# A decoder layer with Strassen weight sums: the copies that begin the sums get a queue of their own, a lead of 24 and other rates

## The chip, the cores and the metric

The kernel runs on one core of one Trainium2 chip. The metric is the device time of one execution in microseconds (us); lower is better. Each time is the median of several executions of the same program. The durations below come from one execution that the hardware profiler recorded.

## The reference

One layer of a decoder, in float32, for one sequence of 512 tokens of width 1024. A combined input projection gives queries, keys and values for three attention mixers and three gate vectors; the branches are projected, gated, summed and projected once more; after a layer norm come a squared-ReLU MLP (1024 to 4096 to 1024) and a gated input embedding, and a second layer norm. Cut to what matters here:

```python
def mixer(x, w_in, ...):
    proj = x @ w_in                                  # 1024 x 8192 columns, 3072 of them gates
    (da_q, da_k, da_v, sb_q, sb_k, sb_v, dl_q, dl_k, dl_v, gates) = jnp.split(proj, ...)
    o_da = diff_attention(...)                       # 4 heads, two softmax maps, T5 bias
    o_sb = stick_breaking_attention(...)             # 8 heads
    o_dl = dilated_attention(...)                    # 3 groups x 4 heads, T5 bias
    g = jax.nn.sigmoid(gates).reshape(B, S, 3, D)
    merged = g[:, :, 0] * (o_da @ w_branch_da) + g[:, :, 1] * (o_sb @ w_branch_sb) \
           + g[:, :, 2] * (o_dl @ w_branch_dil)
    return merged @ w_out

x = layer_norm(ALPHA * x + mixer(x, ...), ln1_g, ln1_b)
c = jnp.square(jax.nn.relu(x @ w_up)) @ w_down
ple = jax.nn.sigmoid(x @ w_ple_gate) * (p @ w_ple)
x = layer_norm(ALPHA * x + c + ple, ln2_g, ln2_b)
```

## The kernel before

**Products.** Every large product is made in split precision: a weight block of 128 x 1024 floats is loaded into `raw`, ScalarE (ACT) rounds it to `wh` (L232), VectorE (DVE) forms the rest `wl = raw - wh` (L235), and TensorE (PE) makes three matmuls with them. There are 4 buffers of `raw` and 7 of `wh` and of `wl`.

**Items.** The work is a list of 312 items; an item is the matmuls of one or of a few blocks and the evacuation of their result. The items run in the order: projections for q, k and v (items 0 to 58, with the attention heads interleaved into them by `step()`), the three gates (59 to 100), the three branch projections (101 to 124), the output projection, embedding gate and embedding (from 125 on, `wout_at`), and then the MLP, in eight groups of up-projection and seven of down-projection. In the loop at the end of `trunk` each item calls `pump`, which starts loads and splits as far ahead as the buffers allow.

**Strassen sums.** Gates, embedding gate and most of the MLP use Strassen-Winograd's scheme: seven products in place of eight. Four of the seven weight operands are sums of blocks. They are not made by an engine but by transfers between DRAM buffers named `total`: `totals()` lists, for each set of four blocks (23 sets), four plain copies of 512 KB (`total<-in_...`, issued on SyncE's queue, SP) and four accumulating transfers (`total<-in_...` or `total<-total`, issued on GpSimd's queue, POOL), 92 copies and 92 additions in all. `add()` (L165) takes the next entry of one list, `sums`, in which copies and additions of a set stand mixed. The loop calls `add()` at a rate: each item adds its `size` to `due[0]`, and each time that reaches `rate` one entry is issued (L1572 to L1577). An addition also waits for a recent cast of a weight (`casts[0]`), so that they don't bunch. `fill()` (L186) issues the loads; before it loads a `total` it issues what is still missing of it.

**Queues.** SP's queue is in order and carries all loads of weights (`raw`), the copies and most other loads. POOL's queue is in order too and carries the additions, the loads and stores of the bias tables, and a few small power operations (L1357, L591). A scheduler places the instructions of each engine; an instruction with `tc.issue_after(i)` stands behind `i` in the order.

**Bias tables.** `tables()` loads three one-hot tables (`oh`, 66 KB each, L1142 to L1144), PE multiplies them with the bias table (L1109), the results go to DRAM (`rv`) and come back shifted (`sh`). It is started at item 13.

Of the kernel before, what the change touches and what calls it, by code (L numbers as in the profile page):

```python
# [13 lines left out]
OP = mybir.AluOpType  # L14
# [38 lines left out]
def trunk(tc, a, out):  # L53
    nc = tc.nc
    es = ExitStack()
    with es:
        big = es.enter_context(tc.tile_pool(name="big", bufs=64))
        ring = es.enter_context(tc.tile_pool(name="ring", bufs=1))
        one = es.enter_context(tc.tile_pool(name="one", bufs=1))
# [7 lines left out]
        def nm(s):  # L67
            uid[0] += 1
            return f"{s}_{uid[0]}"
# [68 lines left out]

        RING, RAW = 7, 4
        ORDERED, AHEAD = 17, 4  # L140
        loads, sums, chunks, placed = [], deque(), [], []
        st = {"dma": 0, "split": 0}

        def load(src, w, own=False):
# [4 lines left out]
        def totals(quads):  # L149

            def new():
                return dram.tile([P, 1024], F32, name=nm("total"), tag=nm("total"), bufs=1)

            t = [[new() for _ in range(4)] for _ in quads]
            for o, i, more in ((0, 0, False), (2, 1, False), (0, 1, True), (2, 3, True), (1, 3, False), (3, 2, False)):
                for (q, x) in zip(quads, t):
                    sums.append((x[o], q[i], more))
            for o in (1, 3):
                for x in t:
                    sums.append((x[o], x[0 if o == 1 else 1][:, :], True))  # L160
            return [{1: q[0], 2: q[2], 3: q[3], 4: x[3], 5: x[0], 6: x[1], 7: x[2]} for q, x in zip(quads, t)]

        casts = deque(maxlen=3)

        def add():  # L165
            if not sums:
                return
            t, s, more = sums.popleft()
            if not more:
                wide = [x.rearrange("(a b) m -> a (b m)", b=4) for x in (t[:, :], s)]  # L170
                nc.sync.dma_start(*wide)
                return
            i = nc.gpsimd.dma_start(t, s, accum_op=OP.add, max_dma_last_dim=2048)  # L173
            tc.add_manual_dep(getattr(i, "ins", i), casts[0].name, mybir.DependencyInfo(
                mybir.DependencyClass.Sync, mybir.DependencyReason.DATA), reason="one sum at a time")

        def chunk_of(s):
            c = {"from": s, "w": s["w"]}
# [7 lines left out]
        def fill():  # L186
            while st["dma"] < len(loads):
                s = loads[st["dma"]]
                while any(t is s["src"] for t, _, _ in sums):
                    add()  # L190
                if not s["own"]:
                    if len(placed) >= RAW and placed[-RAW]["uses"]:
                        break
                    placed.append(s)
                if s["own"]:
                    s["raw"] = slot("rawx")[:, :s["w"]]
                else:
                    r = ring.tile([P, 1024], F32, name=nm("raw"), tag="raw", bufs=RAW)
                    s["raw"] = r[:, :s["w"]]
                if 0 < st["dma"] < ORDERED:  # L200
                    with tc.issue_after(st["load"]):
                        i = nc.sync.dma_start(s["raw"], s["src"])
                else:
                    i = nc.sync.dma_start(s["raw"], s["src"])
                st["load"] = getattr(i, "ins", i)
                if st["dma"] == AHEAD:

                    tc.add_manual_dep(st["load"], st["warm"].name, mybir.DependencyInfo(
                        mybir.DependencyClass.Sync, mybir.DependencyReason.DATA), reason="first loads alone")
                st["dma"] += 1  # L210
# [165 lines left out]
        at = {}  # L376
# [130 lines left out]
        gates_at = len(items)  # L507
# [55 lines left out]
        first_branch = len(items)  # L563
# [490 lines left out]
        wout_at = len(items)  # L1054
# [83 lines left out]
        def tables():  # L1138
            nonlocal tab_g0, tab_g1, tab_g2
            oh = [slot("oh") for _ in range(3)]  # L1140
            ohd = a["onehot"]
            nc.gpsimd.dma_start(oh[0][:33, :], ohd[:, 0:512])  # L1142
            nc.gpsimd.dma_start(oh[1][:33, :], ohd[:, 512:1024])
            nc.gpsimd.dma_start(oh[2][:33, :], ohd[:, 1024:1536])  # L1144
# [398 lines left out]
        for n, it in enumerate(items):  # L1543
# [20 lines left out]
            if n == 13:  # L1564
                pending.append(tables())
# [3 lines left out]
                da_tables()  # L1569
            if n == DA_TABS + 4:  # L1570
                turn_da()
            if n >= 7 and not wout_at + 4 <= n < wout_at + 22:  # L1572
                due[0] += it["size"]
                rate = 2.3 if n < gates_at else 4.5 if n < first_branch else 3
                while due[0] >= rate:
                    due[0] -= rate
                    add()  # L1577
# [116 lines left out]
```

## Time and profile before

| | us |
|---|---|
| median of 3 executions | 1088.29 (1086.98 to 1091.54) |
| the profiled execution, whole | 1088.46 |
| its span, first to last instruction | 1086.8 |
| PE busy in the span | 1052.2 (97%) |
| DVE, ACT, POOL busy | 753.3, 559.1, 105.3 |
| mean granted clock of PE | 0.991 |
| transfers on SP's queue (q1) | 188.15 MB |
| transfers on POOL's queue (q0) | 50.57 MB |

PE is busy nearly throughout, so what remains to be had lies in its few idle stretches and in stretches at a lower clock. The profile lists what each engine waited for; the windows view gives the busy time of each engine, the granted clock and the share of time that the 16 DMA engines were busy, stretch by stretch.

### The profile page before, as it was taken

What the parts mean: (1) busy time and instruction counts of PE and PEld (TensorE: products, weight loads), DVE (VectorE), ACT (ScalarE), POOL (GpSimd) and SP (SyncE); (2) the same over time, 40 slices, a digit from 0 to 9 for tenths busy, and PEclk for the clock granted to TensorE, in tenths of its full rate; (3) what the DMA queues carried; (4) which work ended last, traced back from release to release, by engine and by line L of the source; (5) the groups of instructions that cost most, each with busy time, mean ns of one, the idle gap of its engine ahead of it and who ended that gap; (6) DMA issues with size and microseconds to landing.
All of it is one profiled execution on the core that took longest, in us unless ns stands there. A gap on an engine that the chain in (4) does not pass through costs nothing.

```text
span 1086.8 us, 14845 instructions
## 1 busy us (share of the span) xinstructions
PE 1052.2 (97%) x5503; PEld 899.4 (83%) x5503; DVE 753.3 (69%) x1306; ACT 559.1 (51%) x906; POOL 105.3 (10%) x130
## 2 busy tenths in 40 slices
PE   8999899999999999999999999999999999899997
PEld 5888588999888887788888888878989988778985
DVE  5987367655434656897666675987888667577786
ACT  6665344443332445688654232565856635547551
POOL 0001210110120101011101100100110001000000
PEclk9999899999999999999999999999999999999999
DMA  7676583966888667586989888369999979797622
GB/s 271 205 194 182 162 243 124 266 175 174 219 246 215 173 194 214 197 249 212 262 279 253 231 259 265 117 187 299 285 263 289 298 219 297 258 251 240 218 92 78
DMA packets 73112, 240.58 MB, mean 221 GB/s; under 512 B 8506, under 2 KB 11466, under 8 KB 71568
## 3 DMA queue, kind: packets, MB, share of 16 engines
q1 hardware_dynamic: 46496, 188.15, 47.4%
q0 software_dynamic: 25968, 50.57, 26.3%
q8 instruction: 43, 0.70, 0.3%
q10 hardware_dynamic: 576, 0.92, 0.2%
q14 instruction: 29, 0.24, 0.1%
HBM read 237.48 MB, written 98.59 MB: 309 GB/s over the span
## 4 chain that ended last, share of the span: by engine, by line
PE 79%; DMA 7%; DVE 6%; issue 5%; ACT 3%; POOL 0%; SPq 0%; DVEq 0%; ACTq 0%; POOLq 0%
PE mm L85 5%; PE mm L84 5%; PE mm L86 5%; PE mm L822 4%; PE mm L824 4%; PE mm L823 4%; PE mm L340 3%; PE mm L342 3%; PE mm L341 3%; PE at L430 3%; PE at L428 3%; PE at L431 3%; DMA raw<-total 2%; DVE wl L235 2%; PE mm L548 2%
## 5 line engine op out<-in xcount | busy, mean ns | idle before, releaser
L235 DVE TENSOR_TENSOR wl<-raw,wh 128x1024 fp32r<-128x1024 f32 x245 | 297.2, 1221 | 130.0 <-ACT wh L232 128.0
L232 ACT CAST wh<-raw 128x1024 fp32r<-128x1024 f32 x245 | 256.0, 1050 | 235.8 <-PE mm L85 61.2
L84 PE MATMUL mm<-xhT,wh 128*128 128x512 f32 x304 | 121.0, 398 | 0.0
L86 PE MATMUL mm<-xhT,wl 128*128 128x512 f32 x304 | 120.0, 395 | 0.0
L85 PE MATMUL mm<-xlT,wh 128*128 128x512 f32 x304 | 119.9, 394 | 0.0
L173 POOL DMA_DIRECT2D total<-total x46 | 40.8, 907 | 379.6 <-ACT wh L232 236.7
L822 PE MATMUL mm<-XH,wh 128*128 128x256 f32 x256 | 73.2, 286 | 4.0 <-ACT wh L232 2.1
L824 PE MATMUL mm<-XH,wl 128*128 128x256 f32 x256 | 73.3, 286 | 2.4 <-DVE wl L235 2.4
L823 PE MATMUL mm<-XL,wh 128*128 128x256 f32 x256 | 73.0, 285 | 0.0
L85 PEld LDWEIGHTS mm<-xlT,wh 128*128 128x128 f32 x304 | 57.6, 190 | 12.6 <-issue 1.7
L86 PEld LDWEIGHTS mm<-xhT,wl 128*128 128x128 f32 x304 | 57.5, 189 | 12.0
L84 PEld LDWEIGHTS mm<-xhT,wh 128*128 128x128 f32 x304 | 57.6, 189 | 11.4 <-PE mm L86 0.4
L340 PE MATMUL mm<-wh,xhT 128*128 128x512 f32 x160 | 64.8, 405 | 0.0
L342 PE MATMUL mm<-wh,xlT 128*128 128x512 f32 x160 | 63.2, 395 | 0.0
L341 PE MATMUL mm<-wl,xhT 128*128 128x512 f32 x160 | 62.9, 393 | 0.0
L822 PE MATMUL mm<-xs,wh 128*128 128x256 f32 x192 | 54.9, 286 | 2.5 <-ACT cut L829 2.5
L823 PE MATMUL mm<-xs,wh 128*128 128x256 f32 x192 | 54.5, 284 | 0.0
L824 PE MATMUL mm<-xs,wl 128*128 128x256 f32 x192 | 54.4, 283 | 0.0
L822 PEld LDWEIGHTS mm<-XH,wh 128*128 128x128 f32 x256 | 49.7, 194 | 4.8 <-ACT wh L232 2.3
L824 PEld LDWEIGHTS mm<-XH,wl 128*128 128x128 f32 x256 | 49.7, 194 | 2.8 <-DVE wl L235 2.8
L823 PEld LDWEIGHTS mm<-XL,wh 128*128 128x128 f32 x256 | 49.7, 194 | 0.2
L916 DVE TENSOR_TENSOR xn<-xn,mm 128x512 f32<-128x512 f32 x50 | 34.1, 682 | 19.2 <-PE mm L911 18.9
(421 smaller groups left out, 2544.9 us busy)
## 6 DMA issues: line engine op xcount, KB each, us to landing
raw<-total SPq DMA_DIRECT2D x92, 512.0 KB, 5.5
total<-total POOLq DMA_DIRECT2D x46, 512.0 KB, 10.1
raw<-in_wt_dram SPq DMA_DIRECT2D x38, 512.0 KB, 5.8
total<-in_wu_dram SPq DMA_DIRECT2D x32, 512.0 KB, 7.0
total<-in_wd_dram SPq DMA_DIRECT2D x28, 512.0 KB, 7.1
raw<-in_wd_dram SPq DMA_DIRECT2D x25, 512.0 KB, 5.1
total<-in_wga_dram SPq DMA_DIRECT2D x24, 512.0 KB, 7.7
raw<-in_wu_dram SPq DMA_DIRECT2D x24, 512.0 KB, 5.9
```

Of the source, the lines that this page charges most:

```text
L84: nc.tensor.matmul(ps, wh, xh, start=start, stop=False, skip_group_check=True)
L85: nc.tensor.matmul(ps, wh, xl, start=False, stop=False, skip_group_check=True)
L86: nc.tensor.matmul(ps, wl, xh, start=False, stop=stop, skip_group_check=True)
L173: i = nc.gpsimd.dma_start(t, s, accum_op=OP.add, max_dma_last_dim=2048)
L232: i = nc.vector.tensor_copy(h, raw) if c.get("dve") else nc.scalar.copy(h, raw)
L235: i = nc.vector.tensor_sub(lo, raw, h.bitcast(F32))
L340: nc.tensor.matmul(ps, x1, c["h"][:, s], start=k == 0, stop=False)
L341: nc.tensor.matmul(ps, x1, c["l"][:, s], start=False, stop=False)
L342: nc.tensor.matmul(ps, x2, c["h"][:, s], start=False, stop=k == 7)
L822: nc.tensor.matmul(o, c["h"][:, s], h, start=first, stop=False, skip_group_check=True)
L823: nc.tensor.matmul(o, c["h"][:, s], lo, start=False, stop=False, skip_group_check=True)
L824: nc.tensor.matmul(o, c["l"][:, s], h, start=False, stop=last, skip_group_check=True)
```

## The change

- `totals()` writes copies and additions of a set into two lists, `copies` and `sums`, each in its own order. Number, sizes, sources and targets of the transfers stay.
- `add()` issues a copy as long as fewer than 24 more copies than additions have been issued, otherwise an addition. So the first 24 calls give copies; then copies and additions alternate until the copies are used up.
- A copy is placed with `tc.issue_after(st["load"])`, behind the latest load of a weight. Before, nothing placed it.
- The one-hot tables are loaded on SP's queue in place of POOL's.
- `rate` goes from 2.3 to 1.8 up to the gates, stays at 4.5 in the gates and the first items behind them, goes from 3 to 2.4 in the branches and to 5.5 in the MLP; the pause around the output projection shrinks from 18 items to 15.

```diff
-        loads, sums, chunks, placed = [], deque(), [], []
+        loads, copies, sums, chunks, placed = [], deque(), deque(), [], []
...
-            for o, i, more in ((0, 0, False), (2, 1, False), (0, 1, True), (2, 3, True), (1, 3, False), (3, 2, False)):
-                for (q, x) in zip(quads, t):
-                    sums.append((x[o], q[i], more))
+            for o, i in ((0, 0), (2, 1), (1, 3), (3, 2)):
+                for q, x in zip(quads, t):
+                    copies.append((x[o], q[i]))
+            for o, i in ((0, 1), (2, 3)):
+                for q, x in zip(quads, t):
+                    sums.append((x[o], q[i]))
             for o in (1, 3):
                 for x in t:
-                    sums.append((x[o], x[0 if o == 1 else 1][:, :], True))
+                    sums.append((x[o], x[o // 2][:, :]))
...
+        LEAD = 24
+        moved = [0, 0]
+
         def add():
-            if not sums:
-                return
-            t, s, more = sums.popleft()
-            if not more:
+            if copies and moved[0] < moved[1] + LEAD:
+                moved[0] += 1
+                t, s = copies.popleft()
                 wide = [x.rearrange("(a b) m -> a (b m)", b=4) for x in (t[:, :], s)]
-                nc.sync.dma_start(*wide)
-                return
-            i = nc.gpsimd.dma_start(t, s, accum_op=OP.add, max_dma_last_dim=2048)
-            tc.add_manual_dep(getattr(i, "ins", i), casts[0].name, mybir.DependencyInfo(
-                mybir.DependencyClass.Sync, mybir.DependencyReason.DATA), reason="one sum at a time")
+                with tc.issue_after(st["load"]):
+                    nc.sync.dma_start(*wide)
+            elif sums:
+                moved[1] += 1
+                t, s = sums.popleft()
+                i = nc.gpsimd.dma_start(t, s, accum_op=OP.add, max_dma_last_dim=2048)
+                tc.add_manual_dep(getattr(i, "ins", i), casts[0].name, mybir.DependencyInfo(
+                    mybir.DependencyClass.Sync, mybir.DependencyReason.DATA), reason="one sum at a time")
...
-            nc.gpsimd.dma_start(oh[0][:33, :], ohd[:, 0:512])
+            nc.sync.dma_start(oh[0][:33, :], ohd[:, 0:512])
...
-            if n >= 7 and not wout_at + 4 <= n < wout_at + 22:
+            if n >= 7 and not wout_at + 5 <= n < wout_at + 20:
                 due[0] += it["size"]
-                rate = 2.3 if n < gates_at else 4.5 if n < first_branch else 3
+                rate = 1.8 if n < gates_at else 4.5 if n < first_branch else 2.4 if n < wout_at else 5.5
```

The scheduler turns this into a new order on all engines. Three places of it follow; the lines of the changed kernel are 8 higher behind `add()`.

**The one-hot tables.** POOL's queue before, from the first additions of the gates' weights on (the number behind a name counts buffers; `total_72` to `total_79` belong to the first gate):

```order
L173 DMA total_73<-total_72 256x512
L173 DMA total_77<-total_76 256x512
L173 DMA total_75<-total_73 256x512
L1142 DMA oh_1175<-in_onehot_dram 33x512
L1143 DMA oh_1176<-in_onehot_dram 33x512
L1144 DMA oh_1177<-in_onehot_dram 33x512
L173 DMA total_79<-total_77 256x512
L1112 DMA rv<-rvs_1183 4x512
```

SP's queue now, at the loads of the same part of the projections (`raw_1152` is the load that stood there as `raw_1149`):

```order
L177 DMA total_81<-in_wga_dram 16x8192
L212 DMA raw_1152<-in_wt_dram 128x1024
L177 DMA total_85<-in_wga_dram 16x8192
L177 DMA total_83<-in_wga_dram 16x8192
L1150 DMA oh_1178<-in_onehot_dram 33x512
L1151 DMA oh_1179<-in_onehot_dram 33x512
L1152 DMA oh_1180<-in_onehot_dram 33x512
L212 DMA raw_1237<-in_wt_dram 128x1024
```

The tables left a queue with additions for one with loads and copies. On POOL the first addition now stands behind the transfers of the tables. The first copy, `total_72`, which stood first of all on SP's queue, now stands behind 26 loads. On PE the first matmul that reads a one-hot table has moved back by 27 rows, 20 of them matmuls of 512 columns and 6 of 256.

**The projections beside the dilated heads.** DVE before, at the end of the first dilated head (`pt` is that head's transposed attention, copied from PE's result `at`; `raw_2593` is the load that is now `raw_2607`):

```order
L95 COPY pt_722_2642<-at_2638 128x384
L235 TENSOR_TENSOR wl_2699<-raw_2593,wh_2698 128x1024
L95 COPY pt_729_2684<-at_2679 128x512
L299 COPY dl_k_2754<-mm_2723 128x512
L235 TENSOR_TENSOR wl_2749<-raw_2599,wh_2748 128x1024
L235 TENSOR_TENSOR wl_2783<-raw_2607,wh_2782 128x1024
L299 COPY dl_k_2823<-mm_2792 128x512
L235 TENSOR_TENSOR wl_2818<-raw_2613,wh_2817 128x1024
```

DVE now, where the same four weights are split, at the end of the second dilated head:

```order
L95 COPY pt_792_3057<-at_3053 128x384
L243 TENSOR_TENSOR wl_2713<-raw_2607,wh_2712 128x1024
L243 TENSOR_TENSOR wl_2763<-raw_2613,wh_2762 128x1024
L243 TENSOR_TENSOR wl_2798<-raw_2621,wh_2797 128x1024
L243 TENSOR_TENSOR wl_2834<-raw_2627,wh_2833 128x1024
L307 COPY dl_k_3077<-mm_3033 128x512
L95 COPY pt_800_3093<-at_3088 128x512
```

The splits moved back by one head. On PE, 180 rows stood between the last one that writes `at_2638` and the first that reads `wl_2699`; now 12 rows stand between `at_3053` and `wl_2713`.

**The last third of the MLP.** SP's queue before (`total_156` to `total_163` belong to the last two sets):

```order
L171 DMA total_160<-in_wd_dram 16x8192
L204 DMA raw_8281<-total_138 128x1024
L204 DMA raw_8315<-total_139 128x1024
L171 DMA total_158<-in_wu_dram 16x8192
L204 DMA raw_8353<-in_wu_dram 128x1024
L171 DMA total_162<-in_wd_dram 16x8192
L204 DMA raw_8390<-in_wu_dram 128x1024
L204 DMA raw_8427<-total_141 128x1024
```

Now there are loads alone; 2 copies stand behind the MLP's first load (`raw<-in_wu_dram`), where 20 stood:

```order
L212 DMA raw_8291<-total_138 128x1024
L212 DMA raw_8325<-total_139 128x1024
L212 DMA raw_8362<-in_wu_dram 128x1024
L212 DMA raw_8399<-in_wu_dram 128x1024
L212 DMA raw_8436<-total_141 128x1024
```

DVE before at the splits of these weights (L916 adds a down-projection's result `mm` to the accumulators):

```order
L916 TENSOR_TENSOR xn_5680<-xn_5680,mm_8565 128x512
L235 TENSOR_TENSOR wl_8424<-raw_8281,wh_8423 128x1024
L235 TENSOR_TENSOR wl_8458<-raw_8315,wh_8457 128x1024
L916 TENSOR_TENSOR xn_5682<-xn_5682,mm_8590 128x512
L916 TENSOR_TENSOR xn_5686<-xn_5686,mm_8615 128x512
L235 TENSOR_TENSOR wl_8493<-raw_8353,wh_8492 128x1024
```

and now:

```order
L875 TENSOR_TENSOR hs_8550<-cut_8255,hs_8519 128x512
L924 TENSOR_TENSOR xn_5706<-xn_5706,mm_8493 128x512
L805 TENSOR_TENSOR hl_8587<-cut_8327,hh_8586 128x512
L243 TENSOR_TENSOR wl_8501<-raw_8362,wh_8500 128x1024
L243 TENSOR_TENSOR wl_8514<-raw_8399,wh_8513 128x1024
```

Before, 2 rows of PE stood between the last one that writes `mm_8615` and the first that reads `wl_8493`; now 68 stand between `mm_8493` and `wl_8501`.

The additions behind the first layer norm's power operations on POOL are 25 now and were 28.

More of the change, by code (lines that the diff above doesn't have):

```diff
@@ L188, in fill @@
                 s = loads[st["dma"]]
-                while any(t is s["src"] for t, _, _ in sums):
+                while any(t is s["src"] for t, _ in sums):
                     add()
@@ L1141, in tables @@
             ohd = a["onehot"]
-            nc.gpsimd.dma_start(oh[0][:33, :], ohd[:, 0:512])
-            nc.gpsimd.dma_start(oh[1][:33, :], ohd[:, 512:1024])
-            nc.gpsimd.dma_start(oh[2][:33, :], ohd[:, 1024:1536])
+            nc.sync.dma_start(oh[0][:33, :], ohd[:, 0:512])
+            nc.sync.dma_start(oh[1][:33, :], ohd[:, 512:1024])
+            nc.sync.dma_start(oh[2][:33, :], ohd[:, 1024:1536])
             yield from rel_vec(slice(0, 4), [(oh[0][:33, :], 0, 512), (oh[1][:33, 0:128], 512, 128)])
```

## The prediction

> **What bounds the kernel now.** First the page's busy times, then what PE waited for in the whole span (line, what it waited for, us in total, times, longest).
>
> ```profile
> span 1086.8 us, 14845 instructions
> PE 1052.2 (97%) x5503; PEld 899.4 (83%) x5503; DVE 753.3 (69%) x1306; ACT 559.1 (51%) x906; POOL 105.3 (10%) x130
> ...
> PE at L1109 <- issue: 4.6, 1, 4.6
> PE at L321 <- DVE wh L232: 3.3, 1, 3.3
> PE at L910 <- DVE wl L235: 2.7, 2, 1.5
> PE mm L822 <- ACT cut L829: 2.5, 4, 1.5
> PE mm L824 <- DVE wl L235: 2.4, 2, 1.7
> PE at L1365 <- DVE on L1359: 2.2, 2, 1.6
> PE mm L822 <- ACT wh L232: 2.1, 1, 2.1
> PE mm L822 <- DVE cut L834: 1.8, 1, 1.8
> ```
>
> PE bounds the kernel. The change takes no matmul away, so it can win only PE's idle time and the time at a lower clock. The windows view shows where they lie; columns are the stretch, its length, busy time (and instructions) of PE, weight loads, DVE, ACT and POOL, then PE's granted clock, the DMA engines' busy share and GB/s.
>
> ```profile
> 1.00:40.00 39.00, 35.13 (x146) 26.45 (x147) 28.36 (x51) 28.27 (x42) 1.29 (x6) 0.96 0.77 263
> 40.00:130.00 90.00, 85.42 (x379) 65.83 (x378) 61.51 (x110) 46.31 (x80) 10.73 (x14) 0.94 0.63 178
> 130.00:429.00 299.00, 298.70 (x1490) 258.55 (x1489) 173.30 (x443) 124.93 (x251) 37.68 (x46) 1.00 0.73 202
> 429.00:721.00 292.00, 288.28 (x1354) 238.05 (x1353) 217.33 (x352) 157.85 (x256) 27.92 (x29) 1.00 0.76 231
> 721.00:972.00 251.00, 239.93 (x1514) 217.02 (x1513) 184.13 (x225) 145.07 (x197) 24.69 (x28) 0.99 0.90 269
> 972.00:1073.00 101.00, 98.97 (x594) 88.40 (x593) 78.87 (x107) 54.81 (x78) 1.10 (x2) 1.00 0.52 175
> ```
>
> Three stages lose: the second 4.6 us beside a low clock, the fourth 3.7, the MLP 11.1 up to 972 and 2.0 behind it. In the third, where the projections and the heads run, PE idles 0.3 us. My sums are made against the profiled execution, 1088.46 us: its span and 1.7 around it. It stands 0.17 above the median of the runs, so the forecast serves for both.
>
> **What a moved transfer costs the DMA engines.** Queue rows: packets, MB, share of 16 engines over the span.
>
> ```profile
> q1 hardware_dynamic: 46496, 188.15, 47.4%
> q0 software_dynamic: 25968, 50.57, 26.3%
> ```
>
> q1 took 47.4% of 1086.8 = 515 us for 188 MB, 2.74 us per MB, so a copy of 0.52 MB takes about **1.44 us** of all engines. q0 took 286 us, nearly all for 92 additions: **3.1 us** each.
>
> **Term 1, the start: -1.2 us.** From the timeline of SP and PE (start, duration, what):
>
> ```profile
> 0.81 0.62 SPq L171 DMA_DIRECT2D total<-in_wga_dram  x1
> 1.48 0.57 SPq L204 DMA_DIRECT2D rawx<-in_xT_dram  x1
> ...
> 8.61 1.19 PE L321 MATMUL at<-xhT,wh 128*128 128x512 f32 x2 [3.33 <-DVE wh L232]
> ```
>
> The first copy takes 0.67 us of SP ahead of the first load that PE waits for, and stands in the engines ahead of it with 1.44. Gone, that is 0.7 to 2.1 us; I take 1.2, between them, since part of the copy's writing runs beside the loads. The loads of x remain what PE waits for.
>
> **Term 2, the one-hot tables: -9.7 us.** POOL's and PE's timeline, the landing times of `oh`, and two stretches of windows:
>
> ```profile
> 103.40 1.77 POOL L173 DMA_DIRECT2D total<-total  x2 [7.10 <-ACT wh L232]
> 104.52 1.37 POOL L1142 DMA_DIRECT2D oh<-in_onehot_dram  x1
> ...
> DMA to landing us min/median/max: 9.4/9.6/10.0
> ...
> 114.64 2.29 PE L1109 MATMUL at<-oh,rel 33*4 33x512 f32 x4 [4.58 <-issue]
> ...
> 100.00:110.00 10.00, 10.00 (x46) 8.07 (x44) 6.41 (x12) 3.43 (x5) 3.51 (x5) 1.00 0.82 230
> 114.40:124.60 10.20, 9.96 (x23) 5.32 (x24) 3.41 (x7) 4.80 (x10) 1.67 (x3) 0.50 0.53 146
> ```
>
> The additions wait for a cast until 103.40, the tables queue behind them and land at 114.5, where PE, idle since 110.06, starts. Behind the gap PE runs 10.2 us at a clock of 0.50, 23 matmuls in place of 46: another 5.1 us. Together 9.7. In the new order PE reaches the tables 26 matmuls later; 20 of them are long, and at 46 in 10 us that is 4.4 us for those alone, so about 114.5. On SP the tables stand behind one weight load and two copies. The corresponding load was issued at 104.39:
>
> ```profile
> 104.39 0.33 SPq L204 DMA_DIRECT2D raw<-in_wt_dram  x1
> 104.77 0.77 SPq L171 DMA_DIRECT2D total<-in_wga_dram  x1
> ```
>
> A load in an unloaded stretch takes 3.4 us or so to land (the shortest landing of a `raw` in the MLP, below, is 3.4); with three transfers of 1.44 ahead that is about 112, and no addition shares the engines yet. At the 10.0 that the tables took at worst, issued at 107, it is 117 and a gap of 2.5. I take the whole 9.7 and keep 0 to 9.7 for the range.
> The Trainium skill's page "TensorE: Matmul & The Clock Gate" (part 1, the HAM clock gate) says that about 3.4 us of sustained work bring the full clock back. The trace disagrees here: it shows 10.2 us at 0.50. By the page the clock's part would be 1.7 in place of 5.1, and the forecast 3.4 us later.
>
> **Term 3, the MLP from 906 on: -10.5 us.** DVE's and PE's timeline at one of its gaps, the landings of `raw` from 840 to 960, and the page's groups that split a weight:
>
> ```profile
> 925.18 0.69 DVE L916 TENSOR_TENSOR xn<-xn,mm 128x512 f32<-128x512 f32 x1 [1.55 <-PE mm L911]
> 927.67 0.69 DVE L916 TENSOR_TENSOR xn<-xn,mm 128x512 f32<-128x512 f32 x1 [1.81 <-PE mm L911]
> 928.28 1.22 DVE L235 TENSOR_TENSOR wl<-raw,wh 128x1024 fp32r<-128x1024 f32 x1
> ...
> 929.55 0.39 PE L824 MATMUL mm<-XH,wl 128*128 128x256 f32 x1 [1.68 <-DVE wl L235]
> ...
> DMA to landing us min/median/max: 3.4/6.2/10.3
> ...
> L235 DVE TENSOR_TENSOR wl<-raw,wh 128x1024 fp32r<-128x1024 f32 x245 | 297.2, 1221 | 130.0 <-ACT wh L232 128.0
> L232 ACT CAST wh<-raw 128x1024 fp32r<-128x1024 f32 x245 | 256.0, 1050 | 235.8 <-PE mm L85 61.2
> ```
>
> This is the place with 2 rows of PE between `mm_8615` and `wl_8493`: PE finishes a down-projection, DVE adds it (0.69), splits (1.22), and PE waits 1.68 us. The split's place in DVE's order makes the gap; a late load does so too: with landings up to 10.3 us, a cast of 1.05 and a split of 1.22, four buffers turn once in 12.6 us, 3.1 us per load, and a load is needed for each 24 matmuls of 256 columns, under 3. From 906 to 990 the waits add up to 9.8 us (2.7, 2.4, 2.1, 1.8, 0.6, 0.2), and 3.4 us at half clock cost 1.7:
>
> ```profile
> 937.00:940.40 3.40, 3.40 (x18) 3.40 (x17) 2.56 (x3) 1.38 (x2) 0.00 (x0) 0.50 0.83 272
> ```
>
> Now 18 copies and 3 additions fewer stand in the stretch from 721 to 972: 18 x 1.44 + 3 x 3.1 = 35 us of 251, so the DMA share falls from 0.90 to 0.76. And the splits stand ahead, with 68 rows in place of 2. Of 11.5 I take 10.5; nothing is the other end.
>
> **Term 4, the MLP's first items: -1 us.** From 720 to 760 PE waited 2.9 us for results copied by ACT behind casts whose loads came late. One copy goes; the additions start two items sooner. Ends 0 and -2.9; I take a third.
>
> **Term 5, the differential heads: 0.** PE's 3.6 us there (2.2 at L1365, 1.4 at L1333) come partly from POOL:
>
> ```profile
> 428.84 0.88 POOL L173 DMA_DIRECT2D total<-total  x1 [4.59 <-DMA total<-total]
> 429.43 1.39 POOL L1357 TENSOR_TENSOR ms<-ms,mhalf 128x4 f32<-128x4 f32 x1
> ```
>
> The power operation stands behind an addition that waited 4.6 us. In the new order each of the four stands right behind an addition, two did so before. That can win 2.2 or cost 4.6; I take nothing.
>
> **Term 6, the projections: +3 us.** From 130 to 429, 50 copies stand on SP where 35 stood, and 41 additions on POOL where 36 stood: 15 x 1.44 + 5 x 3.1 = 37 us more in 299, so the share rises from 0.73 to 0.85. Splits lose their lead, at the shown place from 180 rows to 12. Those 12 are 8 transposes, 2 products with values and 2 matmuls at least, some 2 us, against a copy of 0.5 to 0.7 and a split of 1.22: about even, with at most a microsecond lost each time. The MLP, with similar leads, lost 11.5 in its last third. So 0 to 12; nearest is the count of a few places at a microsecond: 3.
>
> The lists, `LEAD` and the same 184 transfers themselves cost nothing: SP and POOL issue as many as before.
>
> **The sum:** 1088.5 - 1.2 - 9.7 - 10.5 - 1 + 0 + 3 = **1069.1 us**, 1.8% faster; by its own bounds 1062 to 1077.
>
> **The rivals.**
> *The tables come late on SP too.* A POOL transfer shares the engines with SP's; on SP it stands behind everything issued there. If `oh` lands past 117, gap and half clock stay: 1079. Against it: PE now needs them 4.4 us later.
> The Trainium skill's page "DMA: Bandwidth & Descriptors" (queues, rings and completion order) says that each engine takes turns between queues and works through one queue in its order; that is this rival's mechanism, and the rows above have no case of it.
> *Additions, not copies, starve the MLP.* 25 of 28 remain. If only a third of term 3 comes: 1076.
> *The projections give it back.* Term 6 at its upper end: 1078; with late tables as well, 1088.
> *Slower.* Between 130 and 429 stand 42 weight loads. If lateness makes a split wait as at 929.55, 1.7 us each time, the 22 us won are gone at 13 loads, and 20 loads cost 34: 1100. For it: 12 rows where 180 stood. Against it: these weights serve 24 long matmuls, 5.3 us, twice the MLP's time per load, and the share stays below 0.90.
> *It doesn't do what it says*: the order shows that the copies moved, so that has little weight.
>
> **How the numbers follow.** Forecast as it stands (1062 to 1077) 0.60; late tables 0.10; additions 0.06; projections 0.10; two of these together, or none of the gains, 0.07, within 0.5% of 1088; slower 0.07. What a measurement can tell from no change is about 0.5%, 5.4 us. Faster by more: 0.60 + 0.10 + 0.06 + 0.08 = 0.84; within 0.09; slower 0.07. The range of eight in ten runs from 1060, all of PE's gaps gone with the best start, to 1084, past the rivals at 1079 and short of the pairs.
>
> **What would show it.** No gap before the first L1117 and a clock of 1.00 from 110 to 125; no half clock in the MLP, waits at L828 to L832 and L917 to L919 under 2 us in all, DMA share near 0.76 there; a share near 0.85 and gaps under 5 us from 130 to 430; PE's first product about a microsecond sooner. Wrong would be: a row `PE at L1117 <- issue` of over 2 us, or waits for `wl` between 200 and 430 that add up to over 10.

## The result, and the profile after

The change made the kernel slower: 1117.64 us median (1116.26 to 1118.53) against 1088.91 of the kernel before (here four executions, one more than in the table above), ratio 1.0261 with a 95% interval of 1.0236 to 1.0286. The forecast was 1069.1, and the range ended at 1084. The profiled execution of the changed kernel has a span of 1114.5 us, 27.7 more than before's. One of the ten executions of run e5 below took 2690.31 us and is left out of that run's median.

First the page's busy times of the changed kernel, then what PE waited for in its whole span (line, what it waited for, us in total, times, longest). The change moves lines from about 160 on down by 8: L1109 is now L1117, L1333 is L1341, L235 is L243.

```profile
span 1114.5 us, 14863 instructions
PE 1060.7 (95%) x5503; PEld 908.1 (81%) x5503; DVE 753.6 (68%) x1306; ACT 558.4 (50%) x906; POOL 103.0 (9%) x127
...
PE at L1341 <- DVE lg L1336: 12.4, 3, 11.9
PE at L135 <- ACT da_ka L126: 9.4, 1, 9.4
PE at L1117 <- issue: 3.7, 1, 3.7
PE mm L830 <- ACT cut L837: 3.7, 1, 3.7
PE mm L436 <- DVE da_qb L105: 3.5, 1, 3.5
PE at L1475 <- DVE L L1459: 2.7, 1, 2.7
PE mm L348 <- ACT wh L240: 1.8, 1, 1.8
...
PE mm L349 <- DVE wl L243: 1.2, 1, 1.2
```

Before's waits in the MLP for `wl` and `wh` are off the list, as forecast; the `wl` and `wh` at its end belong to the projections. At its head stand two waits in the differential attention's heads: for the softmax tile `lg`, 0.9 us before, and for `da_ka`, which before did not have. The windows of the changed kernel show the stages (stretch, length, busy time of PE, weight loads, DVE, ACT, POOL, then PE's granted clock, the DMA share and GB/s), at last the one place alone:

```profile
130.00:429.00 299.00, 291.62 (x1421) 251.08 (x1421) 158.88 (x418) 114.28 (x233) 40.03 (x47) 0.98 0.77 206
429.00:721.00 292.00, 266.72 (x1232) 221.59 (x1231) 189.79 (x308) 138.60 (x228) 28.85 (x32) 0.95 0.81 245
721.00:972.00 251.00, 245.10 (x1498) 219.80 (x1497) 202.92 (x261) 155.72 (x217) 24.63 (x28) 0.99 0.82 232
...
429.00:500.00 71.00, 45.74 (x201) 37.63 (x200) 38.88 (x84) 30.56 (x64) 7.50 (x8) 0.78 0.81 245
```

From 429 to 500 us PE does 201 matmuls where before did 345 (67.62 us busy, clock 1.00). To place the rest, the next table goes by work in place of time: each matmul counts with the median duration of its form, and a row gives how much later (+) or sooner (-) a kernel has done the same share of that work than the kernel before had at the time on the left. It holds the profiled executions of all kernels of this study; e1 to e11 are the experiments below.

```
before  change     e1    e2    e3    e4    e5    e6    e7    e8    e9   e10   e11
  98.6   -3.0    -2.2  -2.4   0.2  -0.7  -3.3  -3.4  -2.4  -0.6  -1.3   0.1  -1.0
 176.3   -2.2     0.9 -10.5  -7.7  -9.9  -3.3  -1.2  -0.2  -9.9 -10.5  -7.4 -10.2
 380.3    2.7     1.2  -9.9  -2.7  -9.8   1.3   5.0   4.9  -9.7 -10.4  -7.4 -10.1
 437.8    8.2    -0.7 -11.4   1.3 -12.0   6.7  35.2   8.8 -12.1 -12.7  -3.8 -12.4
 460.9   39.0    27.7   8.0  33.4  19.7  16.1  34.0  30.7   1.7 -13.0  -2.3 -12.8
 690.1   37.8    26.5   7.1  32.3  18.5  15.8  33.3  29.4   0.6 -12.9  -1.9 -12.3
 759.9   41.8    27.0  11.3  35.5  20.0  16.4  38.1  33.5   0.5 -11.3  -1.7  -9.4
 903.0   41.4    26.6  10.9  35.1  19.6  16.0  37.7  33.0   0.1 -11.8  -1.4  -9.8
1078.8   27.4    12.6  19.4  21.1   5.6   2.0  23.7  19.0  -7.3 -15.7  -3.4 -23.8
```

Read down the column of the change: 3.0 us won at the start; nothing won at the one-hot tables; 4.9 lost up to 380 (one place, at 322 us); 5.5 more up to 438 (7.2 at 401 us, of which some comes back); then **30.8 lost in a single place**, before's 438 to 461; 4 lost at the MLP's beginning; 14.0 won in the rest of the MLP.

The 30.8 add up from PE's own rows: it waits 9.4, 0.5, 11.9 and 3.5 us there, 25.3 in all, and behind the waits it does 13.1 us of work at a granted clock of 0.50 (from 452.1 to 462.3 and from 469.2 to 489.7 us), which costs 6.5 more; before idled 0.8 in that stretch.

That place in the changed kernel, on SP's queue and then on ACT and DVE (start, duration, what, idle time ahead of it and its end):

```profile
443.52 2.59 SPq L212 DMA_DIRECT2D raw<-total  x3
446.17 0.62 SPq L177 DMA_DIRECT2D total<-in_wd_dram  x1
450.96 0.33 SPq L212 DMA_DIRECT2D raw<-total  x1
451.35 0.49 SPq L177 DMA_DIRECT2D total<-in_wu_dram  x1
453.89 0.32 SPq L212 DMA_DIRECT2D raw<-total  x1
454.26 3.04 SPq L493 DMA_DIRECT2D xq<-in_xT_dram  x4
...
454.27 1.04 ACT L240 CAST wh<-raw 128x1024 fp32r<-128x1024 f32 x1 [1.66 <-DMA raw<-total]
455.23 0.58 ACT L122 ACTIVATE da_ka<-mm 64x512 fp32r<-64x512 f32 x1
...
473.41 0.69 DVE L508 TENSOR_TENSOR xq<-xq,xq 128x512 f32<-128x512 f32 x1 [12.61 <-DMA xq<-in_xT_dram]
474.02 0.16 DVE L1329 TENSOR_SCALAR mx<-mx 128x2 f32<-128x2 f32 x1
```

Here the gates' stage reads blocks of x again (`xq`, eight transfers, L493 within `x_load`) for the sums that the seven-product scheme needs. On ACT, casts of weights that arrive late stand ahead of the step that makes `da_ka`; on DVE a subtraction of `xq` stands ahead of the softmax step that PE waits for, and waits 12.61 us for its data. Before, the same stretch of SP's queue ran so:

```profile
415.83 10.75 SPq L204 DMA_DIRECT2D raw<-total  x4
426.69 2.10 SPq L485 DMA_DIRECT2D xq<-in_xT_dram  x4
428.84 0.49 SPq L171 DMA_DIRECT2D total<-in_wu_dram  x1
```

The loads of x went out 27.6 us sooner, though PE was only 8.2 us ahead. And they were faster. For the tile `xq`, first before, then changed:

```profile
DMA to landing us min/median/max: 4.2/7.7/10.2
```

```profile
DMA to landing us min/median/max: 6.7/15.4/17.4
```

So the place has two candidate causes: transfers that crowd each other (copies, additions, six weights and x), or an order in which the splits, and with them the loads behind them on SP, come too late.

### The profile page after: what moved, and what is told of

It reads as the page before. It is cut to its first block, busy times and chain, and to the rows that moved or that the text cites. A ratio compares the mean times of both kernels' runs of the same rounds, so it can differ in the third digit from the quotient of the medians.

```text
span 1114.5 us, 14863 instructions
## 1 busy us (share of the span) xinstructions
PE 1060.7 (95%) x5503; PEld 908.1 (81%) x5503; DVE 753.6 (68%) x1306; ACT 558.4 (50%) x906; POOL 103.0 (9%) x127
## 4 chain that ended last, share of the span: by engine, by line
PE 87%; DVE 5%; DMA 3%; ACT 2%; issue 1%; POOL 0%; DVEq 0%; SPq 0%; ACTq 0%
PE mm L84 6%; PE mm L85 6%; PE mm L86 6%; PE mm L830 5%; PE mm L832 5%; PE mm L831 5%; PE mm L349 3%; PE mm L348 3%; PE mm L350 3%; PE at L436 3%; PE at L438 3%; PE at L439 3%; PE mm L917 2%; PE mm L919 2%; PE mm L918 2%; PE mm L556 2%
## 5 line engine op out<-in xcount | busy, mean ns | idle before, releaser
L243 DVE TENSOR_TENSOR wl<-raw,wh 128x1024 fp32r<-128x1024 f32 x245 | 297.0, 1222 | 133.0 <-ACT wh L240 131.7
L181 POOL DMA_DIRECT2D total<-total x46 | 43.4, 964 | 391.8 <-ACT wh L240 269.4
L348 PEld LDWEIGHTS mm<-wh,xhT 128*128 128x128 f32 x160 | 38.6, 242 | 6.4 <-ACT wh L240 2.3
```

Of the source, the lines that this page charges most:

```text
L243: i = nc.vector.tensor_sub(lo, raw, h.bitcast(F32))
L348: nc.tensor.matmul(ps, x1, c["h"][:, s], start=k == 0, stop=False)
```

## The experiments

The first four undo or do one part each. Theory A was the lead that the order gives to the splits, B the number of transfers ahead of the loads of x, C the fixed place of copies behind a load.

**e1, LEAD 8 in place of 24.**

```diff
-        LEAD = 24
+        LEAD = 8
```

> The changed kernel with LEAD = 8 in place of 24: 16 copies fewer run ahead at the start, every rate as in the change, so that 59 copies (67 in the change, 46 before) stand on SP ahead of the first load of xq. In the instruction order the splits of the weights used between 200 and 400 us stand again some 18 to 26 us of matmuls ahead of their use, where the change has 6 to 17 and the kernel before 18 to 37. Theory A, the lost lead of the splits: most of the 40 us lost between 300 and 490 come back, 1080 to 1095 us. Theory B, too many transfers ahead of the loads of xq: 40 us for 21 copies is 1.9 us each, 8 copies fewer give 15 us, about 1102. Theory C, the copies' fixed place behind a load (issue_after): 1117 as in the change.

Measured: 1102.05 us, ratio 1.0113 (1.0088 to 1.0138). The time is the one that B named, yet by chance, for the table shows another reading. The waits at 322 and 401 us are gone (column e1 stays within 0.9 to 1.2 from 176 to 380), as A said of those splits. 28.4 of the 30.8 us at the reload of x remain, although eight copies fewer stand ahead of it.

**e2, the old rate up to the gates.**

```diff
-rate = 1.8 if n < gates_at else ...
+rate = 2.3 if n < gates_at else ...
```

> The changed kernel with 2.3 in place of 1.8 as the rate up to the gates, all else as in the change: 55 copies ahead of the first load of xq, and splits 22 to 27 us of matmuls ahead of their use between 240 and 400 us. Theory A, the lost lead of the splits: most of the 40 us come back, a few are lost in the MLP, where 12 copies more now fall: 1078 to 1092 us. Theory B, too many transfers ahead of the loads of xq: 12 copies at 1.9 us, 23 us back, about 1095. Theory C, the copies' fixed place behind a load: 1105 or more.

Measured: 1117.20 us, ratio 1.0237 (1.0194 to 1.0279): a miss for A and B. The profiled execution is its quickest, 1108.3; the other three lie at 1117, and what they lost more was not seen. In the profile the first 430 us are 11 ahead of before, the reload loses 19.4, and the MLP, which has 12 copies more, 8.5, most of it in two waits of 7.0 and 5.1 us.

**e3, no fixed place for copies.**

```diff
-                with tc.issue_after(st["load"]):
-                    nc.sync.dma_start(*wide)
+                nc.sync.dma_start(*wide)
```

> The changed kernel without issue_after around a copy, all else as in the change; 67 copies ahead of the first load of xq, the splits' lead between 200 and 400 us as low as in the change (6 to 17 us of matmuls), the first copy again ahead of the loads of x. Theory A, the lost lead of the splits, and theory B, too many transfers: no gain, 1114 to 1122 us, with some 2 us lost again at the start. Theory C, the copies' fixed place behind a load: back to 1080.

Measured: 1110.73 us, ratio 1.0206 (1.0175 to 1.0238). C falls: 32.1 us are lost at the reload. The start's 3 us are gone, as expected; 7.9 are won at the tables, which no theory named.

**e4, the kernel before with the new rates only.**

```diff
-if n >= 7 and not wout_at + 4 <= n < wout_at + 22:
+if n >= 7 and not wout_at + 5 <= n < wout_at + 20:
-rate = 2.3 if n < gates_at else 4.5 if n < first_branch else 3
+rate = 1.8 if n < gates_at else 4.5 if n < first_branch else 2.4 if n < wout_at else 5.5
```

> The kernel before with the rates and the pause of the change and nothing else of it: one list in the old order, no LEAD, no issue_after, the tables on POOL. 56 copies ahead of the first load of xq (46 before, 67 in the change); the splits' lead is as in the kernel before up to 280 us and 22 to 25 us of matmuls from there to 400, and 16 in the whole MLP, as in the change. Theory A, the lost lead of the splits: nothing is lost ahead of 500 us and the MLP's 14 us are won, about 1075 us. Theory B, too many transfers ahead of the loads of xq: 10 copies at 1.9 us against the MLP's 14 us, about 1093. Theory C: about 1075, as by A.

Measured: 1094.04 us, ratio 1.0043 (1.0027 to 1.0059). So the new rates alone carry both sides of the change: 14 us won in the MLP, 31.7 lost at the reload. B as a count is finished: 56 copies ahead (e4) lose more than 59 (e1) and as much as 67. That its time is close to B's 1093 is chance, as with e1. What matters must be near the place, so the next four runs work there.

**e5, nothing issued around the reload.**

```diff
-if n >= 7 and not wout_at + 5 <= ...
+if n >= 7 and not gates_at - 6 <= n < gates_at + 2 and not wout_at + 5 <= ...
```

> The changed kernel with no copy and no addition issued for the eight items from six ahead of the gates to one behind their start, the place where the halves of x are loaded again; they follow later. Order and lead of the splits up to there are those of the change, seven splits in a row on DVE ahead of da_kla included. Between 445 and 485 us the change loses 31 us (waits of 9.4, 0.5, 11.9 and 3.5, and half clock). Theory B2, a pile of transfers at this place (8 copies and 5 additions stood beside 6 weights and the 8 loads of x) makes both late: 25 to 31 us come back, 1087 to 1093. Theory A2, the splits' place in the order of ACT and DVE holds them up: the wait for da_ka stays, at most the 12 us of lg come back, 1105 to 1117.

Measured: 1093.25 us, ratio 1.0031 (1.0001 to 1.0060), at the upper edge of what B2 named; in the profile the place loses 9.4 in place of 30.8. The transfers count, but the wait for `da_ka` stays at half its length, as A2 said of it:

```profile
PE at L135 <- ACT da_ka L126: 4.8, 1, 4.8
...
PE at L1341 <- DVE lg L1336: 1.8, 3, 1.3
```

**e6, x read again six items sooner.**

```diff
-            hook(gates_at - 2 + kp, lambda kp=kp: x_load(kp))
+            hook(gates_at - 8 + kp, lambda kp=kp: x_load(kp))
```

> The changed kernel with the halves of x loaded again six items sooner, nothing else changed; as many transfers in all. In the order the subtraction of xq no longer stands ahead of the softmax step that PE waited for. If the reload of x, issued late, is what hurts: the waits for lg (11.9) and da_qb (3.5) go, with the half clock behind them some 18 us, 1098 to 1103. If a pile of transfers hurts all alike (B2): the weights have 8 loads of x less beside them at the place, but as many copies and additions, and the wait for da_ka stays: the same 1098 to 1103. If the splits' place in the order hurts (A2): the wait moves on to the next split, 1110 to 1120.

Measured: 1111.67 us, ratio 1.0198 (1.0167 to 1.0230). A miss for two of the three: the waits for `lg` and `da_qb` went and one of 21.8 us came, at the work that before did at 403 us in place of 445. There too DVE's subtraction of `xq` stands ahead of a softmax step and waits for its data (PE's wait, then DVE's row):

```profile
PE at L1355 <- ACT da_v L93: 21.8, 1, 21.8
...
434.34 0.69 DVE L508 TENSOR_TENSOR xq<-xq,xq 128x512 f32<-128x512 f32 x1 [23.82 <-DMA xq<-in_xT_dram]
```

The eight loads of x stand now among weights and the five additions of that place and take up to 19 us themselves. Moving the victim moved the collision.

**e7, thin additions.** `now[0]` is the number of the item at hand.

```diff
+                if 50 <= now[0] < 59:
+                    t, s = t[:, :64], s[:, :64]
```

> The changed kernel with the additions of items 50 to 58 cut to 64 of 1024 columns, so that some of the sums of weights are left incomplete; the instruction order of PE, ACT, DVE and SP is the same to the row. About nine additions lose 15 of 16 parts of their 3.1 us of all DMA engines, 26 us. If the additions' traffic is what makes weights and x late at 445 to 485 us: 20 to 31 us come back, 1087 to 1098. If it is the copies, or SP's order: under 8 us, 1110 to 1118. If the splits' place in the order: none.

Measured: 1106.25 us, ratio 1.0138 (1.0097 to 1.0180). With PE, ACT, DVE and SP in the same order to the row, the loads of x land 9 us sooner, and the place loses 21.9 in place of 30.8. This is the cleanest price of the crowd: the additions' share is 9 us, between what was expected if they were the cause (20 to 31) and if they were not (under 8).

**e8, the rates of e4 with a pause.**

```diff
+if n >= 7 and not gates_at - 9 <= n < gates_at + 1 and not wout_at + 5 <= n < wout_at + 20:
```

> The kernel before with the rates of the change up to the gates and behind them (run e4), and no copy and no addition for ten items, from nine ahead of the gates to their first; pause behind the gates' end as in the change. Run e4 was 4 us slower than before: level or ahead by 10 to 12 us everywhere except at the reload of x, where it loses 33, and 14 ahead again in the MLP. Theory B2, the pile: nearly all of the 33 come back, 1062 to 1070 us. Theory A2, the splits' place in the order, which is the same there: 1085 to 1094.

Measured: 1080.98 us, ratio 0.9906 (0.9877 to 0.9935), faster than before, and between the two expectations: 13.8 us are still lost at the reload, with no addition near it and no copy ahead of x.

Both theories held a part. What parts them is the instruction order of DVE between the last softmax step and `da_kla` there. Before (a program's order; waits left out):

```
587 L105 SCALAR_TENSOR_TENSOR da_qa_3880<-mm_3823,da_qa_3880 64x512
588 L105 SCALAR_TENSOR_TENSOR da_qb_3881<-mm_3823,da_qb_3881 64x512
589 L1359 TENSOR_TENSOR on_3889<-at_3661,ms_3662 128x512
590 L95 COPY wT_3899<-at_3896 128x256
591 L235 TENSOR_TENSOR wl_3927<-raw_3801,wh_3926 128x1024
592 L105 SCALAR_TENSOR_TENSOR da_kla_3942<-mm_3901,da_ka_3940 64x512
```

and changed:

```
586 L243 TENSOR_TENSOR wl_3815<-raw_3337,wh_3814 128x1024
587 L243 TENSOR_TENSOR wl_3821<-raw_3416,wh_3820 128x1024
588 L243 TENSOR_TENSOR wl_3829<-raw_3530,wh_3828 128x1024
589 L243 TENSOR_TENSOR wl_3835<-raw_3598,wh_3834 128x1024
590 L243 TENSOR_TENSOR wl_3898<-raw_3818,wh_3897 128x1024
591 L243 TENSOR_TENSOR wl_3952<-raw_3824,wh_3951 128x1024
592 L243 TENSOR_TENSOR wl_4044<-raw_3832,wh_4043 128x1024
593 L105 SCALAR_TENSOR_TENSOR da_kla_3967<-mm_3926,da_ka_3965 64x512
```

A split frees one of four raw buffers; SP, which works in order, holds the next weight until then, and `xq` behind it. What SP waited for from 435 to 476 us in the changed kernel, the two largest:

```profile
SPq L212 <- DVE wl L243: 9.8, 6, 3.0
SPq L212 <- DVE rr L1333: 8.1, 1, 8.1
```

Seven splits in a row, late, put seven weights and x into one bunch. Counted for every kernel but e6, whose loads of x stand elsewhere (splits between the last 128x384 `lg` that DVE makes from `at` and `da_kla`; first `xq` issued and last of the first four landed, less PE's own shift at 437.8, against before's 426.7 and 438.3; loss from 437.8 to 460.9; in e1 and e5, where the trace lacks three of the four landings, the start of the subtraction that waited for them stands for the last):

```
         splits  x issued  x landed  PE lost
before      2       0.0       0.0      0.0
e10         2      -3.6      -1.0      1.5
e9          2       1.8      -1.9     -0.3
e11         2       1.8      -3.4     -0.4
e8          7      14.8      10.9     13.8
e5          8      15.8      12.3      9.4
e2          5      11.5      16.3     19.4
e7          8      19.3      17.6     21.9
e1          7      16.9      24.5     28.4
change      8      19.4      26.9     30.8
e3          8      21.2      27.9     32.1
e4          7      16.5      28.5     31.7
```

Where there are 7 or 8 late splits, x goes out 15 to 21 us late, with the pause as without it. The crowd shows in the landing: 11 and 12 us late with the pause (e8, e5), 18 with thin additions (e7), 24 to 29 without either. With the early order a smaller crowd costs next to nothing: before has four additions and two copies there, e10 the same, where the change has five additions and eight copies. The early order beside a crowd as large as the change's was not run, and no run changed the order alone: the kernels that are compared here differ in other places too.

**e9, the pause begins three items sooner.** In place of e8's 9 items ahead of the gates it begins 12 ahead; the first copies stand behind a load; the last rate is 4.5. In the order the splits are back where they stood before.

```diff
-gates_at - 9 <= n < gates_at + 1
+gates_at - 12 <= n < gates_at + 1
-2.4 if n < wout_at else 5.5
+2.4 if n < wout_at else 4.5
-                nc.sync.dma_start(*wide)
+                with tc.issue_after(st["load"]) if len(sums) >= 182 else ExitStack():
+                    nc.sync.dma_start(*wide)
```

> Run e8 with three edits: the pause begins 12 items ahead of the gates in place of 9, only the first copies (those of the first item that has any) stand behind a load, and the rate behind the gates of the MLP is 4.5 in place of 5.5. In the order the rows of SP at the reload of x are those of the kernel before (the four loads of sums, the eight of x), and the splits' lead between 360 and 400 us is 27 us of matmuls in place of 22. Run e8 lost there 14 us (waits of 4.7, 0.5 and 3.7 and the half clock), 2.6 us at the start and 6.7 at 1000 us, where late sums held up a split. If both the pile and the splits' late place in the order cause the loss at the reload: all of these go, 1081 less 20 us, 1060 to 1066. If the pile alone: the wait for da_ka stays, 1068 to 1074.

Measured: 1074.24 us, ratio 0.9863 (0.9832 to 0.9894). Not the 1060 to 1066 named, because 10 us were lost between about 1003 and 1025 us, behind paused sums that now came late (e11 tests this); but at the reload nothing is lost, and the wait for `da_ka` is gone, as expected if pile and order both act. Of the three edits the rate acts only later; whether the longer pause or the place of the first copies brought the early order back was not run apart.

**e10, only the tables on SP.**

```diff
-            nc.gpsimd.dma_start(oh[0][:33, :], ohd[:, 0:512])
+            nc.sync.dma_start(oh[0][:33, :], ohd[:, 0:512])
```

(and the same for `oh[1]` and `oh[2]`).

> The kernel before with only the one-hot tables issued by SP. In its order they stand behind one weight and one or two copies, not behind five copies as in the change. If the copies ahead of them on SP made the tables late in the change: they land ahead of 112 us here, the wait of 4.6 us and the half clock behind it are gone, and with the rest of the order as before the time is 1078 to 1084, if the reload of x loses nothing; its rows on SP are not quite those of before (three copies ahead of the four loads of sums), which can give back up to 10. If tables on SP are late as such: the wait and the half clock stay, 1087 to 1093.

Measured: 1086.38 us, ratio 0.9984 (0.9965 to 1.0003), no difference. The tables' place wins 7.5 us (a wait of 1.65 is left), as the first theory said; 3.6 go at 422 us, where the power operation on POOL, behind an addition sent at 423.77, keeps DVE and so PE waiting:

```profile
PE at L1365 <- DVE on L1359: 4.4, 2, 3.9
```

**e11, e9 with the paused transfers made up sooner.**

```diff
-rate = 1.8 if n < gates_at else 4.5 if n < first_branch else 2.4 if n < wout_at else 4.5
+rate = 1.8 if n < gates_at else 3.0 if n < first_branch else 2.0 if n < wout_at else 5.0
```

> Run e9 with other rates behind the reload of x, so that the paused transfers are made up sooner: 3.0 in place of 4.5 up to the branches, 2.0 in place of 2.4 up to the output weights, 5.0 behind. Up to 480 us the order is that of e9. In e9, 26 us ahead of the kernel before at 1010 us, PE lost 10 us between 1005 and 1060, where its last sums and weights came late; here the last copy stands 24 rows of SP ahead of the constants of the last layer norm in place of 11. If the late sums were the cause: the 10 us are kept, 1062 to 1066 us. If the rates only move the collision: what is won at the end is lost between 480 and 720 us, where the copies now stand, 1072 to 1078.

Measured: **1064.07 us, ratio 0.9783 (0.9767 to 0.9800)**, the fastest kernel here. (The rows named in the expectation were miscounted; they are 21 and 12.) It keeps what the change was forecast to win: tables, MLP, and no loss at the reload.

```profile
429.00:500.00 71.00, 69.60 (x350) 57.48 (x349) 62.40 (x135) 57.51 (x115) 7.78 (x8) 1.00 0.73 216
721.00:972.00 251.00, 250.32 (x1646) 230.78 (x1647) 196.51 (x236) 160.83 (x215) 15.92 (x18) 1.00 0.83 255
```

## Why the prediction was wrong

The terms as forecast, and as the table of work has them:

| term | forecast us | measured us |
|---|---|---|
| 1, start | -1.2 (-0.7 to -2.1) | -3.0 |
| 2, one-hot tables | -9.7 (0 to -9.7) | +0.8 |
| 3, MLP from 906 | -10.5 (0 to -11.5) | -14.0 |
| 4, MLP's first items | -1 (0 to -2.9) | +4.0 |
| 5 and 6, projections and differential heads | +3 (-2.2 to +16.6) | +40.0 |

The rest to 27.4 is 0.4 won between 760 and 903 us.

**Terms 5 and 6 are the step that failed.** Of their 40.0 us, 10.4 were lost up to before's 438 us, where term 6 counted, and 30.8 at the reload of x, in the stretch of term 5, which was put at nothing because only POOL's power operations were weighed there (1.2 were won behind it). Term 6 looked at the right thing, the splits' lead that falls from 180 rows to 12, and priced each place at "at most a microsecond", from a copy of 0.5 to 0.7 us on SP and a split of 1.22. That is the price of one copy ahead of one split. Three things were left out. First, the lead was read at one place in place of along the whole stage: at the reload of x eight splits stand late, and the first load of x goes out 19.4 us late. Secondly, on SP behind those weights stand the eight loads of `xq`, which appear in no term, though the rows of the order held them. Thirdly, ACT and DVE work in order, so that one late weight or block of x holds the softmax and `da_ka` behind it (12.61 us at the subtraction of `xq`). At 322 and 401 us smaller losses occurred, 5.1 and 7.2 us with the clock's loss. At 401 it is the plain case of the term: PE waits 1.8 us for a cast and 1.2 for a split. At 322 it waits for no split. There 22 matmuls of the projections stood before between a dilated head's product with `fold` and its first transposition, while DVE worked on the head's softmax; in the new order none does, and PE idles 0.9 and 2.7 us. e5 and e6, which have the change's order there, show the wait of 2.69 us at the first place again, and e5 the 1.9 at the second; e1, with the lead restored, loses nothing at either. Those 12 us alone are the upper end of term 6.

The range did not follow from the terms either. Added up at their own ends they reach from 1060 to 1104 us, not from 1062 to 1077; the part that the terms allowed to go wrong was cut off, and even 1104 falls short of the 1117.6 measured.

The **slower rival** had the sign, from too many late splits at 1.7 us each, 13 or more. Its test, waits for `wl` of over 10 us between 200 and 430, did not come true (1.2). The loss was one pile-up, and not many small waits; its weight of 0.07 was far too low for an order whose leads had been seen to fall.

**Term 2** failed by its rival, which came true: the tables were late on SP too, and the row `PE at L1117 <- issue` of over 2 us, named as a sign of being wrong, is there with 3.7. SP issued them at 109.24, behind two loads and four copies since 103.94, and PE used them from 116.01 (the trace has no landing of theirs); the last row is e10's:

```profile
106.83 1.87 SPq L177 DMA_DIRECT2D total<-in_wga_dram  x2
109.24 0.36 SPq L1150 DMA_DIRECT2D oh<-in_onehot_dram  x1
...
116.01 1.23 PE L1117 MATMUL at<-oh,rel 33*4 33x512 f32 x4 [3.71 <-issue]
...
117.59:131.24 13.65, 13.65 (x34) 7.99 (x33) 6.94 (x13) 6.11 (x14) 6.21 (x9) 0.50 0.54 202
...
112.26 1.23 PE L1109 MATMUL at<-oh,rel 33*4 33x512 f32 x4 [1.65 <-DMA oh<-in_onehot_dram]
```

The forecast had one load and two copies ahead of them, issue at 107 and PE at the tables at 114.5. PE was there at 112.3, for the 3.0 us won at the start had brought it forward. In e10, issued at 104.87 with no copy right ahead, the place wins 7.5. e2 and e3, with copies ahead on SP but issue at 106.16 and 106.81, win 8.1 and 7.9. In e4, with the tables left on POOL, it wins 9.2: they went out at 98.20, as the addition ahead of them had gone at 95.23. But e1, with two loads and two copies ahead and issue at 107.41, close to the forecast, loses 3.1: PE used the tables 11.6 us later, with additions issued at 103.37 and 111.63 beside them. So neither queue is late as such: the time of issue counts, and in e1 probably the transfers beside it. The Trainium skill's page "DMA: Bandwidth & Descriptors" (queues, rings and completion order) says that each engine works through one queue in order. No run here separates that from the time of issue: from issue to PE's use the tables took 6.8 us in the change and 7.4 in e10.

The clock's part was forecast by the trace's 10.2 us at 0.50; behind the change's wait of 3.7 it was 13.65. The page "TensorE: Matmul & The Clock Gate" of the Trainium skill (part 1, the HAM clock gate), with about 3.4 us of sustained work until full clock, is not borne out here either: PE was busy for all of the 13.65 us.

**Term 3** was right in place and sign: the MLP's waits for splits are gone, 14.0 us where 11.5 had been the most; e4 shows the same 14.0 with the rates alone. Which of its two reasons did it, fewer copies or earlier splits, was not run apart, but the number of copies does not decide by itself: of before's 20 behind the MLP's first load the change leaves 2, e4 10 and e11 16, and all three win 14.0, while e2 with 14 loses 8.5. The DMA shares named as signs, near 0.76 here and 0.85 from 130 to 430, came out at 0.82 and 0.77, in windows that hold earlier work than before's. **Term 1** was right and too small, since the half clock of 3.4 us behind the first product went as well; e3, without the fixed place, wins nothing there. **Term 4** turned round: waits of 1.0 to 3.7 us remain, and no run shows what makes them.

Not settled: why the scheduler puts the splits late when more transfers are called for in items 47 to 49 (e8 against e9) was only seen in its result, the order. The copies' share of the crowd was not run by itself: with only the copies stopped, the list lets more additions through. And the two lists with their LEAD were not measured alone; e1 and e4 bound them.

## What to carry to other kernels

Where a change moves transfers, follow the order along the whole stage for each weight or block that is loaded, and ask at the worst place, not at a typical one, what is behind it on every in-order queue. A transfer that is held by a buffer holds everything issued behind it, so that a few splits placed late can cost much: in this kernel seven or eight late splits with a crowd cost 28 to 32 us, with the background transfers paused 9 to 14, and early splits beside a smaller crowd 0 to 2. Stopping background transfers around a stage that reads fresh data paid here: with the new rates alone (e4) the kernel was 0.4% slower than before, with the pause (e8) 0.9% faster, and with a longer pause, the first copies behind a load and the paused transfers made up sooner (e11) 2.2% faster.

## What the runs showed of the hardware that was not expected

SP took its transfers in this program only as older ones landed: each is given one of eight semaphores in turn, and in the changed kernel the issues at 111.05, 112.23, 113.64, 114.99 and 115.95 us each followed the landing of the transfer eight rows ahead (110.98, 112.21, 113.62, 114.92, 115.94) within 0.07 us. In the two kernels, none of the 620 transfers for which the trace has the landing of the last one with the same semaphore, nearly always eight rows ahead, went out before it. So a run of copies on SP costs not only the 1.44 us of the engines that were counted, but makes the load eight rows further wait for its landing, and x at the reload went out in pieces: two sets of four that took 3.04 and 9.49 us of SP to issue, against 2.10 for the first set before.
